# A hybrid decoder layer on one core: the recurrence's value projection by Strassen's scheme, with the copies of later stages moved

## The chip, the core and the metric

The kernel runs on one core of one Trainium2 chip. The metric is the device time of one execution, in microseconds (us). TensorE (PE) multiplies matrices; VectorE (DVE), ScalarE (ACT) and GpSimd (POOL) work on tiles; SyncE (SP) and POOL issue most of the DMA transfers. An L with a number is a line of the kernel before.

## The reference

One layer of a decoder: 512 tokens, 1024 channels, float32 throughout.

```
h  = RMSNorm(x)                          # 512 x 1024
P  = h @ W_in                            # one product, its columns split into
                                         #   q, f, i, z_a           (1024 each, recurrence)
                                         #   c_q, c_kv, k_rope, z_b (attention)
                                         #   g                      (2 x 1024, merge gates)
y_a = recurrence(q, f, v = i) * silu(z_a)        # 8 heads of 128, chunks of 32 tokens
y_b = latent attention(c_q, c_kv, k_rope) * silu(z_b)   # 8 heads, causal
m   = sigmoid(g_a) * (y_a @ W_pa) + sigmoid(g_b) * (y_b @ W_pb)
out = RMSNorm(x + m @ W_out)
```

The columns i of `W_in` give the recurrence's values: `v = h @ W_i`, 512 x 1024 by 1024 x 1024. This product is what the change rewrites.

## The kernel before, in words

**Products in three parts.** A float32 operand is held as two tiles: a high part, rounded to the type that PE multiplies fast, and a low part, what is left. A product is high x high, high x low and low x high, so three matmuls stand for one (mm3, L99). `hT` holds both parts of h, transposed. Weights come through `load_w` (L110): one DMA of 512 KB into one of three raw buffers, a cast on ACT for the high part (L129), and a subtraction on DVE for the low part (L130). There are four buffers for high parts and four for low parts, and three raw ones, so a load starts when the low part of the load three before it is done.

**The stages.** First x is normalised and transposed, and the small columns of attention are projected (the c stage, to L433; five transposed tiles `cT` and one `kpe` come out of it through PSUM banks of the pool `ax`, L422 to L432). Then come four pairs of recurrence heads (`hg_pair`, L585), then eight attention heads (L959), the two merge gates, the projection of y_a, the projection of y_b, and the output product. The gates, the projection of y_a and the output product already go by Strassen's scheme, in Winograd's form: seven products of quarter blocks instead of eight, paid for by sums of blocks.

**A recurrence pair** projects f (`proj_ch`, 48 matmuls), and both heads' decays, prefix products and keys follow on DVE and POOL (`hg_forget`, L459 to L490: on DVE a scaling, a scan, a reciprocal and three products a head). Pairs 0 and 2 then project 512 columns of values with `proj_tok` (L151, called on L603), 96 matmuls of 512 columns each: for each of four token tiles, eight slices of channels, three parts. A pair's values serve it and the next pair. Then come q, the gate z_a, the states, scores and outputs.

**Sums for Strassen's scheme.** `early_sums` (L816) makes four sums of blocks of h, half at a time, during pair 0: it adds the two parts of a block (L823), subtracts, splits into parts again and stores to DRAM (L830); the gates read them back much later (L1002). Sums of weight blocks are made in DRAM. A `BlockSums` copies four blocks of a weight matrix into DRAM tiles (`start`, L790; eight copies of 512 KB each for two gates, the projection of y_a and the output matrix, 32 in all) and adds other blocks onto them with accumulating DMAs from POOL (`add`, L795). The copies wait in the list `queued`; `load_w` takes one from it behind each plain load and issues it on SP (L124 to L126). The adds are taken one by one at calls of `step` (L845) from the list `adds` (L842).

**Order.** Except where a block says `manual_schedule`, a planner orders each engine's instructions ahead of time by readiness in its own model, with earlier program lines first; `issue_after` puts instructions behind a given one on its engine. On the chip each engine then works strictly in that order.

PSUM has eight banks: three in the pool `mm` and five in the pool `ax`.

Of the kernel before, what the change touches and what calls it, by code (L numbers as in the profile page):

```python
# [18 lines left out]
P = 128  # L19
D = 1024  # L20
# [18 lines left out]
def hybrid_layer(ctx: ExitStack, tc: tile.TileContext, a):  # L39
# [68 lines left out]
    queued = []  # L108

    def load_w(*pieces, to=None):  # L110
# [4 lines left out]
        for src in pieces:  # L115
# [6 lines left out]
            else:  # L122
                last_dma[0] = nc.sync.dma_start(raw[:, o : o + n].rearrange("p (k c) -> p k c", k=src.shape[1]), src)
# [4 lines left out]
            o += n  # L128
        last_hi[0] = nc.scalar.copy(hi[:, :o], raw[:, :o])  # L129
# [51 lines left out]
    kpe = Pair(cpool.tile([P, 2, S], F32R, "kpe")[:])  # L181
    cw = Pool("cwork", "right")
# [23 lines left out]
    x_sb = [st.tile([P, D], F32, "x", bufs=NT) for _ in range(NT)]  # L206
# [50 lines left out]
    def squares(t):  # L257
        sq = st.tile([P, D], F32, "sq", bufs=2)
        nc.scalar.activation(sq[:], x_sb[t][:], AF.Square, accum_out=rss[t][:, 0:1])
        power(rss[t][:, 0:1], rss[t][:, 0:1], 1.0 / D, EPS, neg_half[:, 0:1])  # L260
# [17 lines left out]
    def c_product(t, kh, kind, ks=range(4)):  # L278
# [3 lines left out]
        for k in ks:  # L282
            nc.tensor.matmul(ps, hT[l][:, 4 * kh + k, t * P : t * P + P], c_hl[kh][r][:, k * 256 : k * 256 + 256],  # L283
                             start=kh == 0 and kind == 0 and k == 0, stop=kh == 1 and kind == FIN and k == 3)

# [7 lines left out]
    with tc.manual_schedule(engines={mybir.EngineType.PE, mybir.EngineType.Activation, mybir.EngineType.DVE}):  # L293
# [49 lines left out]
        for t in range(1, NT):  # L343
            if t + 2 < NT:
                squares(t + 2)
            for kh in range(2):
                lo[kh]()
# [49 lines left out]
    c_second += [load_c2(j) for j in range(2, 4)]  # L397
    for t in range(NT):
# [4 lines left out]
        nc.scalar.copy(c_sb[:, t, 256:704], ps[:, 0:448])  # L403
    css = cw.tile([P, 2, NT], F32, "css")
# [31 lines left out]
    ya = ypool.tile([P, H, S], F32, tag="ya", name="ya")  # L436
    ma_pool = Pool("mla_a", "right")
    qtab = ma_pool.tile([P, 2, S], F32, "qtab")
    nc.gpsimd.dma_start(qtab[:], a["c_qtab"])
# [144 lines left out]

    def hg_pair(pair, in_forget=None, in_query=None, before_gate=None, last=None):  # L585
# [3 lines left out]
        if pair:  # L589
            step()  # L590
        else:
            early_sums(kh[0])
# [7 lines left out]
        if pair % 2 == 0:  # L600
            for t in range(NT):
                v_sb[t] = hw.tile([P, 512], F32, f"v{t}")
            proj_tok(w_in, COL_I + cc, hT, lambda t, ps: nc.scalar.copy(v_sb[t][:], ps[:]))  # L603
        else:
# [3 lines left out]
        step()  # L608
# [4 lines left out]
        if pair % 2 == 0:  # L613
# [156 lines left out]
    kh = [slice(0, 2), slice(2, 4)]  # L770
    half_t = [slice(0, 256), slice(256, 512)]
    blocks = lambda t: (t[:, 0:4, half_t[0]], t[:, 4:8, half_t[0]], t[:, 0:4, half_t[1]], t[:, 4:8, half_t[1]])
    TERMS = ((0, 0), (1, 1), (0, 1), (1, 0))

    def minus(out, x, y):
        nc.vector.tensor_tensor(out, x, y, op=ALU.subtract)

    def minus_minus(out, x, y):

        nc.vector.scalar_tensor_tensor(out, x, -1.0, y, op0=ALU.mult, op1=ALU.subtract)  # L780

    class BlockSums:
# [7 lines left out]
        def start(self):  # L790
            for t, ij in zip(self.t, TERMS):
                for q in kh:
                    queued.append(lambda t=t[:, q], w=self.w[ij][:, q]: nc.sync.dma_start(t, w))

        def add(self, *ns):  # L795
            with tc.issue_after(last_pool[0].ins):
                for n in ns:
                    x = {0: self.w[0, 1], 2: self.w[1, 1], 1: self.t[0], 3: self.t[1]}[n]
                    for q in kh:
                        nc.gpsimd.dma_start(self.t[n][:, q], x[:, q], accum_op=ALU.add)  # L800
# [13 lines left out]
    h_dram = [[dram.tile([P, 4, 256], F32, name=f"h{n}{i}") for i in range(2)] for n in range(1, 5)]  # L814

    def early_sums(q):  # L816

        E = lambda tag: ma_pool.tile([P, 2, 256], F32, tag)[:]
        h11, h12, h21, h22 = zip(*[[b[:, q] for b in blocks(t)] for t in hT])

        def whole(tag, hl):
            out = E(tag)
            nc.vector.tensor_tensor(out, hl[0].bitcast(F32), hl[1].bitcast(F32), op=ALU.add)  # L823
            return out

        def keep(n, tag, src):
            hl = Pair(ma_pool.tile([P, 2, 2, 256], F32R, tag)[:])
            split(*hl, src)
            for i in range(2):
                nc.sync.dma_start(h_dram[n - 1][i][:, q], hl[i].bitcast(F32))  # L830

# [428 lines left out]
```

## Time and profile before

| | us |
|---|---|
| median of 3 runs | 609.52 (609.49 to 610.1) |
| the profiled execution | 609.93 |
| its span, first to last instruction | 607.7 |
| PE busy in the span | 598.3 |
| DVE, ACT, POOL busy | 436.6, 286.2, 146.4 |

The span starts at 0 in all times below. The stages, as the trace has them: normalisation and c stage to 45 us, recurrence pairs from 45 to 281, attention from there to 407, the gates and the projection of y_a to 519, the projection of y_b to 562, the output product to 601. DMA moved 114.37 MB, 90 of them on the hardware queue that SP feeds and 22.6 on the software queue that POOL feeds.

### The profile page before, as it was taken

What the parts mean: (1) busy time and instruction counts of PE and PEld (TensorE: products, weight loads), DVE (VectorE), ACT (ScalarE), POOL (GpSimd) and SP (SyncE); (2) the same over time, 40 slices, a digit from 0 to 9 for tenths busy, and PEclk for the clock granted to TensorE, in tenths of its full rate; (3) what the DMA queues carried; (4) which work ended last, traced back from release to release, by engine and by line L of the source; (5) the groups of instructions that cost most, each with busy time, mean ns of one, the idle gap of its engine ahead of it and who ended that gap; (6) DMA issues with size and microseconds to landing.
All of it is one profiled execution on the core that took longest, in us unless ns stands there. A gap on an engine that the chain in (4) does not pass through costs nothing.

```text
span 607.7 us, 9766 instructions
## 1 busy us (share of the span) xinstructions
PE 598.3 (98%) x3670; PEld 524.8 (86%) x3670; DVE 436.6 (72%) x684; ACT 286.2 (47%) x533; POOL 146.4 (24%) x253
## 2 busy tenths in 40 slices
PE   8999999999999999999999999999999999999995
PEld 5998888888888888888888888899999999888884
DVE  7717989599764548959767776747757678567886
ACT  6555245333313342435646555438757854424452
POOL 3106322254350137414254530400000000000012
PEclk9999999999999999999999999999999999999998
DMA  7549479987969967573369575866665564695113
GB/s 257 177 138 345 154 218 369 320 220 171 237 151 275 220 185 147 125 172 90 57 163 169 148 152 126 237 243 198 189 184 178 195 195 160 200 347 183 61 35 139
DMA packets 74543, 114.37 MB, mean 188 GB/s; under 512 B 7512, under 2 KB 41726, under 8 KB 74496
## 3 DMA queue, kind: packets, MB, share of 16 engines
q1 hardware_dynamic: 65244, 89.95, 46.1%
q0 software_dynamic: 8336, 22.55, 19.9%
q10 hardware_dynamic: 916, 1.25, 0.6%
q8 instruction: 29, 0.48, 0.3%
q14 instruction: 18, 0.15, 0.1%
HBM read 105.34 MB, written 39.85 MB: 239 GB/s over the span
## 4 chain that ended last, share of the span: by engine, by line
PE 96%; ACT 1%; DMA 1%; DVE 0%; issue 0%; SPq 0%; POOLq 0%; POOL 0%; ACTq 0%
PE mm_ps L102 19%; PE mm_ps L104 19%; PE mm_ps L103 19%; PE ax_ps L898 16%; PE ax_ps L1096 5%; PE mm_ps L898 3%; PE mm_ps L283 2%; PE ax_ps L757 1%; PE ax_ps L731 1%; PE ax_ps L559 1%; PE mm_ps L1096 1%; PE ax_ps L561 1%; PE ax_ps L521 1%; DMA w_raw<-w_in 1%; PE ax_ps L104 1%; PE ax_ps L103 1%
## 5 line engine op out<-in xcount | busy, mean ns | idle before, releaser
L130 DVE TENSOR_TENSOR w_lo<-w_raw,w_hi 128x1024 fp32r<-128x1024 f32 (+3 forms) x116 | 138.3, 1205 | 68.3 <-ACT w_hi L129 65.4
L129 ACT CAST w_hi<-w_raw 128x1024 fp32r<-128x1024 f32 (+3 forms) x116 | 115.1, 1005 | 130.1 <-PE mm_ps L103 56.5
L102 PE MATMUL mm_ps<-hT,w_hi 128*128 128x512 f32 x320 | 125.8, 394 | 0.0
L103 PE MATMUL mm_ps<-hT,w_hi 128*128 128x512 f32 x320 | 125.3, 391 | 0.0
L104 PE MATMUL mm_ps<-hT,w_lo 128*128 128x512 f32 x320 | 125.2, 393 | 0.0
L104 PEld LDWEIGHTS mm_ps<-hT,w_lo 128*128 128x128 f32 x320 | 60.1, 188 | 12.3
L102 PEld LDWEIGHTS mm_ps<-hT,w_hi 128*128 128x128 f32 x320 | 60.2, 188 | 11.9
L103 PEld LDWEIGHTS mm_ps<-hT,w_hi 128*128 128x128 f32 x320 | 60.2, 188 | 11.9
L898 PE MATMUL ax_ps<-s,w_hi 128*128 128x256 f32 x384 | 54.2, 283 | 0.2 <-ACT w_hi L129 0.2
L898 PEld LDWEIGHTS ax_ps<-s,w_hi 128*128 128x128 f32 x384 | 49.6, 192 | 0.5 <-ACT w_hi L129 0.5
L1147 POOL TENSOR_SCALAR ssum<-ssum 128x1 f32<-128x1 f32 x3 | 0.9, 309 | 188.0 <-ACT sq L1134 188.0
L103 PE MATMUL mm_ps<-w_lo,hT 128*128 128x512 f32 (+1 forms) x96 | 36.6, 383 | 0.0
L104 PE MATMUL mm_ps<-w_hi,hT 128*128 128x512 f32 (+1 forms) x96 | 36.5, 382 | 0.0
L102 PE MATMUL mm_ps<-w_hi,hT 128*128 128x512 f32 (+1 forms) x96 | 36.2, 386 | 0.0
L739 ACT ACTIVATE p<-ax_ps,sm 128x128 f32<-128x128 f32 (+3 forms) x32 | 16.7, 525 | 35.4 <-DVE sm L738 32.8
L741 POOL TENSOR_SCALAR p<-p,sm 128x128 f32<-128x128 f32 (+3 forms) x28 | 15.6, 560 | 66.2 <-DVE sm L740 54.9
L898 PE MATMUL ax_ps<-s,w_lo 128*128 128x256 f32 x192 | 31.4, 284 | 0.0
L469 DVE RECIPROCAL tf<-pr 128x512 f32<-128x512 f32 x8 | 26.8, 3348 | 0.1
L898 PEld LDWEIGHTS ax_ps<-s,w_lo 128*128 128x128 f32 x192 | 26.6, 192 | 0.2 <-DVE w_lo L130 0.2
L102 PE MATMUL mm_ps<-cT,w_hi 128*128 128x512 f32 x52 | 20.7, 397 | 0.0
L104 PEld LDWEIGHTS mm_ps<-w_hi,hT 128*128 128x128 f32 x96 | 18.0, 188 | 3.0
L102 PEld LDWEIGHTS mm_ps<-w_hi,hT 128*128 128x128 f32 x96 | 18.0, 188 | 2.9
(308 smaller groups left out, 1204.8 us busy)
## 6 DMA issues: line engine op xcount, KB each, us to landing
w_raw<-w_in SPq DMA_DIRECT2D x54, 512.0 KB, 6.4
g_t<-w_in SPq DMA_DIRECT2D x16, 512.0 KB, 9.1
w_raw<-g_t SPq DMA_DIRECT2D x16, 512.0 KB, 4.4
g_t<-w_in POOLq DMA_DIRECT2D x8, 512.0 KB, 10.5
pa_t<-w_proj_a SPq DMA_DIRECT2D x8, 512.0 KB, 8.9
g_t<-g_t POOLq DMA_DIRECT2D x8, 512.0 KB, 9.5
out_t<-w_out SPq DMA_DIRECT2D x8, 512.0 KB, 8.0
s<-h POOLq DMA_DIRECT2D x8, 512.0 KB, 11.6
```

The costliest lines, as they stand in the source:

```text
L102: nc.tensor.matmul(ps, lh[lsl], rh[rsl], start=start, stop=False)
L103: nc.tensor.matmul(ps, lh[lsl], rl[rsl], start=False, stop=False)
L104: nc.tensor.matmul(ps, ll[lsl], rh[rsl], start=False, stop=stop)
L129: last_hi[0] = nc.scalar.copy(hi[:, :o], raw[:, :o])
L130: last_lo[0] = nc.vector.tensor_tensor(lo[:, :o], raw[:, :o], hi[:, :o].bitcast(F32), op=ALU.subtract)
L283: nc.tensor.matmul(ps, hT[l][:, 4 * kh + k, t * P : t * P + P], c_hl[kh][r][:, k * 256 : k * 256 + 256], start=kh == 0 and kind == 0 and k ...
L469: nc.vector.reciprocal(rp[:], pr[:])
L521: nc.tensor.matmul(sps[:, sl], kt_[:, sl], v_sb[i][:, (h % 4) * P : (h % 4) * P + P], start=True, stop=True)
L739: last_act[0] = nc.scalar.activation(p[:, :n], sps[:, :n], AF.Exp, scale=SCALE, bias=sm[:, 1:2], accum_out=sm[:, 2:3])
L741: scaled_p = (nc.vector if final else nc.gpsimd).tensor_scalar(p[:, :n], p[:, :n], sm[:, 3:4], 0.5, op0=ALU.mult, op1=ALU.mult)
L898: nc.tensor.matmul(ps[:, o], w[k // 2][i][:, k % 2, cols], ap[j][:, k], start=not banks and c == 0 and n == 0, stop=n == 11, skip_group_ch ...
L1096: nc.tensor.matmul(ps[:, o : o + n], ap[i][:, k, t * P : t * P + P], w[k // 2][j][:, k % 2, o : o + n], start=fresh and c == 0, stop=c == ...
```

## The change: what it does

**Values.** `v = h @ W_i` goes by the same form of Strassen's scheme: h in four blocks of 256 tokens by 512 channels, W_i in four of 512 by 512. `v_product` is one of its seven products: two token tiles, each with 12 matmuls of 512 columns. Pair 0 runs five of them (`values_first`), which give all tokens of the first 512 columns and four partial tiles (`v_late`) that are kept in SBUF; pair 2 runs the other two (`values_rest`). The first partial sum `u` accumulates over four products in two banks of `ax`; before, the values used banks of `mm`.

**Sums of h.** `early_sums` runs once, on whole blocks, in the c stage, behind the last low part of that stage. Sums 2 and 3 stay in SBUF for pair 0, sums 1 and 4 are stored by POOL's queue at once and fetched again for pair 2. Stores of sums 2 and 3 join `queued`.

**Sums of W_i.** Two are made in SBUF, in the buffer of y_a: four loads on SP, two accumulating DMAs on POOL and two additions on DVE in the c stage, two additions on DVE in pair 0, and for pair 2 two more loads and two accumulating DMAs (`RestSum`). x, at the start, lies in that buffer too.

**Transfers.** The 32 copies join `queued` at the end of pair 0's values, behind four stores; after pair 0 six fetches go ahead of them. Two entries go behind each load up to pair 1, one from pair 2 on. The adds for the y_a projection and the output matrix go into attention; the last two heads before the final one issue two steps each. The table `qtab` is loaded after pair 2.

**Order in pairs.** Pairs 1 to 3 project z_a before q; only pair 0 has it after the states.

The core of the diff:

```diff
-                if queued:
+                for _ in range(min(len(queued), behind[0])):
                     with tc.issue_after(last_dma[0].ins):
                         queued.pop(0)()
...
-    x_sb = [st.tile([P, D], F32, "x", bufs=NT) for _ in range(NT)]
+    x_sb = [ya[:, 2 * t : 2 * t + 2].rearrange("p k c -> p (k c)") for t in range(NT)]
...
+    def save(n, q, hl):
+        (nc.gpsimd if n in (1, 4) else nc.sync).dma_start(h_dram[n - 1][:, :, q], hl.both.bitcast(F32))
...
+        e22, e21, e11 = whole("e22", h22), whole("e21", h21), whole("e11", h11)
+        minus(e22, e22, e21)
+        keep(1, e22)
+        minus_minus(e22, e22, e11)
+        s2 = keep(2, e22)
+        minus(e21, e11, e21)
+        s3 = keep(3, e21)
+        e12 = whole("e12", h12)
+        minus_minus(e12, e12, e22)
+        keep(4, e12)
...
+    for q in kh:
+        nc.sync.dma_start(i_w3[:, q], i_w[0, 1][:, q])
+    for q in kh:
+        nc.gpsimd.dma_start(i_w3[:, q], i_w[1, 1][:, q], accum_op=ALU.add)
+    for q in kh:
+        nc.sync.dma_start(i_w2[:, q], i_w[0, 0][:, q])
...
+    with tc.issue_after(c_lo_last.ins):
+        s_kept = early_sums()
+        for q in kh:
+            nc.vector.tensor_tensor(i_w2[:, q], i_w2[:, q], i_w3[:, q], op=ALU.add)
...
+    def v_product(ap, w, done, banks=None, tile=ax_tile):
+
+        res = banks or [tile() for _ in range(2)]
+        for t, ps in enumerate(res):
+            for n, (x, k) in enumerate((x, k) for x in range(3) for k in range(4)):
+                i, j = ((0, 0), (1, 0), (0, 1))[x]
+                nc.tensor.matmul(ps[:], ap(i, k, t), w[k // 2][j][:, k % 2], start=not banks and n == 0, stop=n == 11,
+                                 skip_group_check=banks is not None)
+            done(t, ps)
+        return res
...
+        u = v_product(h11, i_block(0, 0), lambda t, ps: nc.scalar.copy(v_sb[t][:], ps[:]))
+        v_product(s2, i_split(i_w2), late(2), u)
+        v_product(s3, i_split(i_w3), late(3), u)
+        w10, raws = [], []
+        for q in kh:
+            w10.append(load_w(i_w[1, 0][:, q]))
+            nc.vector.tensor_tensor(i_w2[:, q], i_w2[:, q], last_raw[0].rearrange("p (k c) -> p k c", k=2), op=ALU.add)
+        v_product(h12, w10, lambda t, ps: nc.vector.tensor_tensor(v_sb[t][:], v_sb[t][:], ps[:], op=ALU.add), tile=mm_tile)
+        v_product(h22, i_split(i_w2), lambda t, ps: nc.scalar.copy(v_sb[2 + t][:], ps[:]), u)
+        for n, hls in zip((2, 3), s_kept):
+            for q, hl in zip(kh, hls):
+                queued.append(lambda n=n, q=q, hl=hl: save(n, q, hl))
+        for w in (*gate_w, pa_w, out_w):
+            w.start()
...
+        r = v_product(of_sum(s_late[1]), i_split(i_w2), rest(3), tile=mm_tile)
+        v_product(of_sum(s_late[4]), i_block(1, 1), rest(2), r)
...
-            proj_tok(w_in, COL_I + cc, hT, lambda t, ps: nc.scalar.copy(v_sb[t][:], ps[:]))
-        else:
+            (values_rest if pair else values_first)()
+        if pair:
             zz = gate()
...
+    adds = [(gate_w[0], 0), (RestSum(),), (gate_w[0], 1), (gate_w[0], 2), (gate_w[0], 3), (gate_w[1], 0), (gate_w[1], 1),
+            (gate_w[1], 2), (gate_w[1], 3), None, (pa_w, 0), (pa_w, 1), (pa_w, 2), (pa_w, 3),
+            (out_w, 0), (out_w, 1), (out_w, 2), (out_w, 3)]
...
     for pair in range(H // 2 - 1):
+        if pair == 2:
+            behind[0] = 1
         hg_pair(pair)
         if pair == 0:
-            early_sums(kh[1])
+            fetch_rest()
     early = []
+    qtab = ma_pool.tile([P, 2, S], F32, "qtab")
+    nc.gpsimd.dma_start(qtab[:], a["c_qtab"])
...
-            step()
+            for _ in range(1 + (h > 4)):
+                step()
```

`rest(n)` finishes a tile of values on DVE, straight from the bank: minus the bank, plus the kept partial tile.

More of the change, by code (lines that the diff above doesn't have):

```diff
@@ L284, in c_product, with minus, minus_minus, kept @@
                              start=kh == 0 and kind == 0 and k == 0, stop=kh == 1 and kind == FIN and k == 3)
+    kh = [slice(0, 2), slice(2, 4)]
+    half_t = [slice(0, 256), slice(256, 512)]
+    blocks = lambda t: (t[:, 0:4, half_t[0]], t[:, 4:8, half_t[0]], t[:, 0:4, half_t[1]], t[:, 4:8, half_t[1]])
+    TERMS = ((0, 0), (1, 1), (0, 1), (1, 0))
+    def minus(out, x, y):
+        nc.vector.tensor_tensor(out, x, y, op=ALU.subtract)
+    def minus_minus(out, x, y):
+        nc.vector.scalar_tensor_tensor(out, x, -1.0, y, op0=ALU.mult, op1=ALU.subtract)
+    h_dram = [dram.tile([P, 2, 4, 256], F32, name=f"h{n}") for n in range(1, 5)]
+    i_v = w_in[:, COL_I : COL_I + D].rearrange("(k p) c -> p k c", p=P)
+    i_w = {(i, j): i_v[:, 4 * i : 4 * i + 4, 512 * j : 512 * j + 512] for i in range(2) for j in range(2)}
+    i_w3, i_w2 = ya[:, 0:4], ya[:, 4:8]
+    KEEP = {1: ("qn", "kn"), 2: ("qn", "kn"), 3: ("qp", "qtab"), 4: ("qp", "qtab")}
+    def kept(n):
+        return [Pair(ma_pool.tile([P, 2, 2, 256], F32R, tag)[:]) for tag in KEEP[n]]
+    def save(n, q, hl):
+        (nc.gpsimd if n in (1, 4) else nc.sync).dma_start(h_dram[n - 1][:, :, q], hl.both.bitcast(F32))
+    def early_sums():
+        es = Pool("early", "left")
+        h11, h12, h21, h22 = zip(*[blocks(t) for t in hT])
+        def whole(tag, hl):
+            out = es.tile([P, 4, 256], F32, tag)[:]
+            nc.vector.tensor_tensor(out, hl[0].bitcast(F32), hl[1].bitcast(F32), op=ALU.add)
+            return out
+        def keep(n, src):
+            hls = kept(n) if n in (2, 3) else [Pair(es.tile([P, 2, 2, 256], F32R, f"s{i}")[:]) for i in range(2)]
+            for q, hl in zip(kh, hls):
+                split(*hl, src[:, q])
+                if n in (1, 4):
+                    save(n, q, hl)
+            return hls
+        e22, e21, e11 = whole("e22", h22), whole("e21", h21), whole("e11", h11)
[8 more added lines that the diff above has]
+        keep(4, e12)
+        es.close()
+        return s2, s3
     w_c1 = w_in[:, COL_C + 256 : COL_C + 704].rearrange("(k p) c -> p k c", p=P)
@@ L345, in hybrid_layer @@
                 squares(t + 2)
-            for kh in range(2):
-                lo[kh]()
+            for n in range(2):
+                lo[n]()
             if t + 1 < NT:
@@ new lines, in hybrid_layer, with add, fetch_rest @@
+    s_late = {}
+    class RestSum:
+        def add(self):
+            with tc.issue_after(last_pool[0].ins):
+                for q in kh:
+                    nc.gpsimd.dma_start(i_w2[:, q], i_w[0, 1][:, q], accum_op=ALU.add)
+    def fetch_rest():
+        items = [lambda q=q: nc.sync.dma_start(i_w2[:, q], i_w[0, 0][:, q]) for q in kh]
+        for n in (1, 4):
+            s_late[n] = kept(n)
+            for q, hl in zip(kh, s_late[n]):
+                items.append(lambda n=n, q=q, hl=hl: nc.sync.dma_start(hl.both.bitcast(F32), h_dram[n - 1][:, :, q]))
+        queued[0:0] = items
@@ L612, in hg_pair @@
             before_gate()
-        if pair % 2 == 0:
+        if not pair:
             zz = gate()
```

92 lines of the change are left out of this document (46 added, 46 removed).

## The prediction

> **What bounds the kernel now.** I read the page's busy times first, then the chain that ended last, then what PE waited for.
>
> ```profile
> PE 598.3 (98%) x3670; PEld 524.8 (86%) x3670; DVE 436.6 (72%) x684; ACT 286.2 (47%) x533; POOL 146.4 (24%) x253
> ...
> PE 96%; ACT 1%; DMA 1%; DVE 0%; issue 0%; SPq 0%; POOLq 0%; POOL 0%; ACTq 0%
> ```
>
> ```profile
> PE ax_ps L248 <- DVE zero L294: 1.2, 1, 1.2
> PE mm_ps L283 <- ACT hT L274: 0.6, 1, 0.6
> PE ax_ps L898 <- ACT w_hi L129: 0.2, 1, 0.2
> PE ax_ps L272 <- DVE xn L264: 0.2, 1, 0.2
> ```
>
> PE is the bound: it works 98% of the span, the chain is 96% PE, and its waits on other engines are 2.2 us together. So time falls only by matmuls taken away, and each microsecond for which PE is made to wait comes back in full. Next, the windows of the pairs (span, then busy time of PE, PEld, DVE, ACT, POOL, then the granted clock, the DMA engines' busy share and GB/s; the boundaries lie at each pair's outputs), and two stretches inside them.
>
> ```profile
> 54.00:113.50 59.50, 59.50 (x352) 49.70 (x351) 53.16 (x70) 23.87 (x36) 18.11 (x29) 1.00 0.83 261
> 113.50:160.30 46.80, 46.80 (x302) 39.62 (x301) 37.00 (x43) 14.58 (x33) 20.61 (x38) 1.00 0.89 229
> 160.30:218.30 58.00, 58.00 (x352) 48.68 (x351) 36.86 (x43) 19.14 (x38) 15.93 (x34) 1.00 0.92 229
> ```
>
> ```profile
> 58.20:80.50 22.30, 22.30 (x102) 18.38 (x101) 22.30 (x26) 8.60 (x13) 7.29 (x18) 1.00 0.48 169
> 82.00:122.00 40.00, 40.00 (x266) 33.85 (x265) 29.60 (x43) 15.20 (x33) 13.07 (x12) 1.00 1.05 328
> ```
>
> PE never pauses here. But in pair 0 DVE has 53.16 us of work in 59.5, and while the first values run (58.2 to 80.5) it has no free moment. ACT has less than half. The DMA engines are full from 82 to 122 and PE does not notice. So what the change asks of DVE in pair 0 matters most, then what it asks of the DMA engines.
>
> **What is taken from PE.** Before, the values are 2 x 96 = 192 matmuls of 512 columns (`proj_tok`, four token tiles by eight slices by three parts). After, seven products of 24, 168. The price comes from a run of 24 such matmuls, 512 columns wide, in the output product:
>
> ```profile
> 562.41 5.44 PE ax_ps L1096 x24
> ```
>
> That is 0.227 us each, 5.44 us a product. A matmul's own row shows 0.39 us because neighbours overlap; 96 of them at 0.227 give 21.8 us, which with four transposes fills the 22.3 of the window above. The 24 matmuls fewer are 5.44 us. Nothing is added on PE. Pair 0's values become 27.2 us instead of 21.8, pair 2's 10.9 instead of 21.8.
>
> **Sums of h, moved to the c stage.** The rows of DVE there (start, duration, and in brackets the idle time before):
>
> ```profile
> 42.97 3.50 DVE L130 TENSOR_TENSOR w_lo<-w_raw,w_hi 128x1024 fp32r<-128x1024 f32 x3 [12.19 <-ACT w_hi L129]
> 49.29 1.23 DVE L130 TENSOR_TENSOR w_lo<-w_raw,w_hi 128x1024 fp32r<-128x1024 f32 x1 [2.82 <-ACT w_hi L129]
> 50.44 2.59 DVE L421 TENSOR_SCALAR c_sb<-c_sb,css 128x384 f32<-128x384 f32 x8
> 53.65 1.23 DVE L130 TENSOR_TENSOR w_lo<-w_raw,w_hi 128x1024 fp32r<-128x1024 f32 x1 [0.61 <-ACT w_hi L129]
> 54.79 0.54 DVE L464 TENSOR_SCALAR f<-tf,c,c 128x512 f32<-128x512 f32 x1
> 56.22 1.23 DVE L468 TENSOR_TENSOR_SCAN pr<-f,fr 128x512 f32<-128x512 f32 x1 [0.89 <-POOL fr L465]
> 57.37 0.73 DVE L427 SCALAR_TENSOR_TENSOR cT<-ax_ps,par,cT 128x512 fp32r<-128x512 f32 x1
> 58.01 3.34 DVE L469 RECIPROCAL tf<-pr 128x512 f32<-128x512 f32 x1
> 61.27 2.63 DVE L427 SCALAR_TENSOR_TENSOR cT<-ax_ps,par,cT 128x512 fp32r<-128x512 f32 x4
> 63.81 1.22 DVE L130 TENSOR_TENSOR w_lo<-w_raw,w_hi 128x1024 fp32r<-128x1024 f32 x1
> 64.94 0.69 DVE L486 TENSOR_TENSOR ki<-k,tf 128x512 f32<-128x512 f32 x1
> 65.55 0.69 DVE L823 TENSOR_TENSOR qr<-hT,hT 128x512 f32<-128x512 f32 x1
> 66.15 0.69 DVE L823 TENSOR_TENSOR qs<-hT,hT 128x512 f32<-128x512 f32 x1
> 66.75 0.69 DVE L823 TENSOR_TENSOR qh<-hT,hT 128x512 f32<-128x512 f32 x1
> 67.35 0.68 DVE L823 TENSOR_TENSOR p<-hT,hT 128x512 f32<-128x512 f32 x1
> 67.96 0.68 DVE L172 TENSOR_TENSOR kpe<-ax_ps,kpe 128x512 fp32r<-128x512 f32 x1
> ```
>
> Two operands of 1024 elements cost 1.17 us in a row (3.50 for three), of 512 elements 0.60 (65.55 to 66.15). The sums are eight operations of 1024 and eight low parts of 512, and two additions of weights follow: 10 x 1.17 + 8 x 0.60 = 16.5 us. DVE stands idle for the 12.19 us before 42.97, so they start near 30.8 and end near 47.3. The eight casts on ACT, at 0.6 each, lie beside. The first projection's low parts, begun at 42.97 before, then begin at 47.3, and the first is there at 48.4:
>
> ```profile
> 46.01 0.40 PE L104 MATMUL mm_ps<-hT,w_lo 128*128 128x512 f32 x1
> ...
> 58.22 0.39 PE L102 MATMUL mm_ps<-w_hi,hT 128*128 128x512 f32 x1
> ```
>
> PE uses that low part at 46.01, so it could stand 2.4 us; or it does its 16 matmuls on the high part first (3.6 us, to 48.7) and nothing is lost. DVE's later idle time (2.82 and 0.61) absorbs the shift. The old sums leave pair 0: 24 operations of 512, 14.4 us of DVE's work there.
>
> POOL issues the stores of sums 1 and 4 itself. Those of sum 4 fall due near 46 and may stand ahead of the roots for which L421 waits:
>
> ```profile
> L800 POOL DMA_DIRECT2D g_t<-w_in x8 | 9.7, 1436 | 0.0
> ```
>
> Two issues at 1.44 put L421 off by up to 2.9 us, from 50.4 to 53.3. That costs nothing as long as DVE is on low parts until 52.0 (47.3 + 4 x 1.17) anyway; without that cover the transposes of the c tiles, next on PE, come up to 2.9 late, inside the bound of the next part.
>
> **DVE's account in pair 0.** A head's six steps on DVE are in the rows above: 0.54 (L464), 1.23 (L468), 3.34 (L469) and three products at 0.69 (L486).
>
> A head is 7.2 us. From 47.3 without a pause: four low parts (f and the first product) 4.7, L421 2.6, cT 3.4, kpe 0.6, two heads 14.4, and eight more low parts and two additions for the products two to five, 10 x 1.17 = 11.7. That is 37.4 us, so the last low part is there at 84.7. PE's plan: values from 58.2, a product each 5.44, four transposes of 0.45, so the fifth starts at 80.4; its 11th matmul is the first that needs that part, 2.3 us in: 82.7. DVE is late by about 2 us, and PE waits for it. The bounds: if both heads go before the third product's weights, these are ready at 47.3 + 25.7 + 4.7 = 77.7, needed at 69.5 + 2.3 = 71.8, and PE loses 6; if the second head goes behind them, 0. The row at 63.81, a low part between the first head's steps, shows that weights do slip ahead; I take the balance of the whole account, 2.0.
>
> A second way to the same wait: the first product now opens a bank of `ax`. All five hold the transposed c tiles until DVE has read them (L427), and kpe's transposes want the first to come free. By the rows 57.37, 58.01 and 61.27 a second bank comes free at 61.9, behind a reciprocal: 3.7 us after 58.2. If the four reads go before the reciprocal it is about 58.7. PE waits once, and DVE goes on meanwhile, so this and the low parts do not add; the larger counts, and 0 to 6 holds for both.
>
> **Pair 2.** A bank of `values_rest` must be read by DVE before the second product may add to it, 2.7 us after its last matmul. A reciprocal of 3.34 before the 0.68 of the read makes it 1.3 late: 0 to 1.3, and I take 0.5. DVE's 36.86 of 58.0 us become, with four reads of 0.68, 39.6 of 47.1; that fits. ACT gets six casts of weights more in the kernel, beside its 47%: nothing. In attention POOL issues 16 accumulating DMAs instead of 12, and POOL is busy 24%: nothing on the path.
>
> **Transfers.**
>
> ```profile
> q1 hardware_dynamic: 65244, 89.95, 46.1%
> q0 software_dynamic: 8336, 22.55, 19.9%
> ```
>
> So 512 KB (0.524 MB) takes 0.461 x 607.7 x 0.524 / 89.95 = 1.63 us of all 16 engines on SP's queue, and 2.81 on POOL's. In the c stage four loads, two accumulating transfers and four stores from POOL, 4 x 1.63 + 6 x 2.81 = 23.4 us, take the place of three copies (4.9):
>
> ```profile
> 30.80:42.97 12.17, 12.17 (x62) 11.29 (x61) 0.00 (x0) 5.62 (x17) 0.00 (x0) 1.00 0.47 166
> ```
>
> ```profile
> 28.03 0.39 SPq L123 DMA_DIRECT2D w_raw<-w_in  x1
> ```
>
> Half of the DMA engines' time is free there. SP may issue the four loads ahead of the first projection's, which then land up to 6.5 us later (4 x 1.63). The second of those was asked for at 28.03, and PE begins with the first at 45, so I take nothing; were one late, its whole delay would be PE's. The full stretch 82:122 cost PE nothing either, so I take 0 of a range up to 6.0 (below).
>
> **The sum.** On the profiled execution: 609.93 - 5.44 + 2.0 + 0.5 = 607.0. It lies 0.41 above the median of the runs, 609.52, so the forecast for the median is 606.6.
>
> **Rivals.** *All covers hold.* The planner puts the second head behind the weights and the reads before the reciprocal. For: no PE wait in any pair before, with DVE full. Time 609.52 - 5.44 = 604.1.
>
> *DVE swallows the gain.* Heads first, as earlier lines go first: a wait of 4.3 to 6.6 us with pair 2's share, 608.3 to 610.8, no change, near 609.5. For: DVE works without a pause from 58.2 to 80.5 already, and it trails its work there: kpe's low part runs at 67.96, though its cast on ACT ended at 62.2. Against: 63.81.
>
> ```profile
> 61.59 0.59 ACT L171 CAST kpe<-ax_ps 128x512 fp32r<-128x512 f32 x1 [2.36 <-PE ax_ps L431]
> ```
>
> *Loads stand behind copies in pair 1: slower.* Pair 1 has six loads, and two entries go behind each: 18 x 1.63 + 6 accumulating x 2.81 = 46.2 us of DMA in 46.8 us of PE. For the pair before the same account gives 12 x 1.63 + 16.9 = 36.5, and the row shows 0.89 x 46.8 = 41.7, so 1.14 times as much; 52.8 then, 6.0 over. If the last loads wait for all of it, with DVE's 2.5 in other pairs: 609.52 - 5.44 + 2.5 + 6.0 = 612.6. It decides once loads come more than 4.2 us late altogether. Against: three raw buffers let a load start long before use, and the stretch at 1.05 did no harm. [...]
>
> ```profile
> w_raw<-w_in SPq DMA_DIRECT2D x54, 512.0 KB, 6.4
> ```
>
> That is 6.4 us from issue to landing where 1.63 is its own transfer. [...]
>
> **How the numbers follow.** A measurement of this kernel can tell about 0.2%, 1.2 us, from no change. Forecast, a PE wait of 1 to 4.2 us (605.1 to 608.3): 0.40. All covers hold: 0.25. DVE swallows it: 0.19. Loads late: 0.16. Faster is the first two, 0.65; same 0.19; slower 0.16. The range leaves out the lower edge of the cover case and the upper part of the slow one: 603.9 to 611.0.
>
> **What would show it.** Right: 168 matmuls of the values in the matmul groups, PE's busy time down by about 5; DVE without idle time from 31 to 85; a PE wait of 1 to 4 us between 58 and 85 put down to a low part (DVE) or to the release of a bank, none in pair 1; DMA share near 1 in pair 1. Wrong: PE waits in pair 1 or 2 on w_raw, by way of ACT's casts; a c stage that ends later than 45; or PE without any wait, which would mean that DVE's order put weights first.

## The result: slower, 619.5 us against 609.5

The changed kernel takes 619.51 us (median; 618.15 to 621.69) where the kernel before takes 609.52 (609.49 to 610.1). The ratio is 1.0166, interval 1.0155 to 1.0178. The forecast was 606.6, in a range of 603.9 to 611.0. The profiled execution after is 619.51 us, its span 617.7 against 607.7. From here on an L with a number is a line of the kernel whose rows are shown; the changed kernel's L132, for instance, is L130 before.

First the page of the changed kernel (busy times, granted clock by slices of 15.4 us, the chain), then all that PE waited for.

```profile
PE 599.4 (97%) x3646; PEld 524.2 (85%) x3646; DVE 449.8 (73%) x692; ACT 291.0 (47%) x539; POOL 158.3 (26%) x261
...
PEclk9999699999999999998999999999999999999998
...
PE 79%; DMA 6%; DVE 5%; POOL 3%; issue 3%; ACT 2%; SPq 1%; POOLq 0%; ACTq 0%; DVEq 0%
```

```profile
PE ax_ps L496 <- DVE c_sb L492: 2.9, 1, 2.9
PE ax_ps L102 <- DVE k L634: 2.7, 1, 2.7
PE ax_ps L502 <- DVE cT L498: 1.8, 1, 1.8
PE ax_ps L252 <- DVE zero L354: 1.2, 1, 1.2
PE ax_ps L588 <- ACT kt L580: 0.8, 1, 0.8
PE mm_ps L104 <- DVE w_lo L132: 0.8, 1, 0.8
PE ax_ps L664 <- DVE cT L498: 0.6, 1, 0.6
```

The 24 matmuls are gone (3670 to 3646), yet PE is busy 1.1 us longer: it ran some of the others at a lower clock, in slices 5 and 19 (0.6 and 0.8 in the line PEclk). The chain is 79% PE where it was 96%. The waits stand in two places. The windows of the pairs, cut at their outputs as in the prediction:

```profile
54.00:128.20 74.20, 68.81 (x375) 56.68 (x374) 54.42 (x64) 27.10 (x37) 16.62 (x38) 0.93 0.68 233
128.20:176.50 48.30, 47.49 (x304) 39.95 (x303) 34.09 (x43) 14.93 (x32) 21.93 (x38) 1.00 0.76 183
176.50:228.90 52.40, 52.40 (x327) 44.45 (x326) 40.33 (x48) 17.95 (x36) 18.37 (x35) 1.00 0.91 244
```

PE stood idle for 5.4 us of pair 0's window, at a mean clock of 0.93; for 0.8 in pair 1's, and not at all in pair 2's. PE's rows with a wait (in brackets) show where: the first of them still ahead of that window, the other three, 5.4 together, in it. The rows of POOL and DVE show why. There kd holds the rotary products of attention's shared key, and css the roots by which DVE scales the c tiles (c_sb):

```profile
46.51 0.50 PE L104 MATMUL mm_ps<-hT,w_lo 128*128 128x512 f32 x1 [0.79 <-DVE w_lo L132]
61.03 1.97 PE L496 MATMUL ax_ps<-ident,c_sb 128*128 128x128 f32 x8 [2.94 <-DVE c_sb L492]
64.83 1.09 PE L502 MATMUL ax_ps<-ident,kd 128*128 128x128 f32 x4 [1.83 <-DVE cT L498]
66.53 3.78 PE L664 MATMUL ax_ps<-w_hi,hT 128*128 128x512 f32 x8 [0.62 <-DVE cT L498]
```

```profile
46.03 5.71 POOL L485 TENSOR_TENSOR kd<-c_sb,ktab 128x256 f32<-128x256 f32 x1 [6.55 <-ACT c_sb L470]
...
56.67 1.11 POOL L179 TENSOR_TENSOR css<-css,fixed 128x4 f32<-128x4 f32 x1
```

```profile
49.85 1.28 DVE L174 TENSOR_TENSOR s<-e,s 128x512 fp32r<-128x512 f32 x2
51.26 1.56 DVE L132 TENSOR_TENSOR w_lo<-w_raw,w_hi 128x1024 fp32r<-128x1024 f32 x1
55.69 1.55 DVE L492 TENSOR_SCALAR c_sb<-c_sb,css 128x384 f32<-128x384 f32 x4 [2.87 <-POOL css L179]
57.16 1.21 DVE L174 TENSOR_TENSOR w_lo<-ya,w_hi 128x1024 fp32r<-128x1024 f32 x1
58.29 3.46 DVE L492 TENSOR_SCALAR c_sb<-c_sb,css 128x256 f32<-128x256 f32 x4
```

The same kd product and the roots in the kernel before:

```profile
45.90 1.17 POOL L414 TENSOR_TENSOR kd<-c_sb,ktab 128x256 f32<-128x256 f32 x1 [27.84 <-ACT c_sb L403]
...
49.25 2.30 POOL L177 TENSOR_TENSOR css<-css,fixed 128x4 f32<-128x4 f32 x2
```

From kd's start to the second root POOL took 5.7 us before and takes 11.8 now. DVE is through with its sums and low parts at 52.8, then stands 2.87 us for the roots, which POOL works out behind kd. The scaling of the c tiles ends at 61.75, so their transposes, and all behind them on PE, come late. And PE is at half clock when it starts again (windows; the last three numbers are granted clock, DMA share, GB/s):

```profile
62.00:64.00 2.00, 1.00 (x5) 0.59 (x3) 2.00 (x3) 1.27 (x2) 0.00 (x0) 0.50 0.14 57
...
70.00:72.00 2.00, 2.00 (x7) 1.58 (x7) 1.97 (x2) 0.23 (x1) 0.72 (x6) 0.68 0.00 0
```

The second place is the start of attention. The rows of SP's queue show out_t's copies among the loads, two issues held for 5.3 and 4.1 us (0.37 when free); ACT then waits 9.60 us for a load, its squares come late, and PE waits for k, again with half clock behind it:

```profile
259.30 5.29 SPq L124 DMA_DIRECT2D w_raw<-w_uq  x1
264.63 4.12 SPq L937 DMA_DIRECT2D out_t<-w_out  x1
```

```profile
272.59 1.04 ACT L131 CAST w_hi<-w_raw 128x1024 fp32r<-128x1024 f32 x1 [9.60 <-DMA w_raw<-w_in]
```

```profile
282.00:284.00 2.00, 0.85 (x2) 0.75 (x3) 0.73 (x2) 1.64 (x6) 1.57 (x3) 0.72 0.04 12
284.00:286.00 2.00, 2.00 (x6) 1.41 (x6) 2.00 (x6) 0.00 (x0) 0.00 (x0) 0.50 0.00 0
```

The account of the span: 24 matmuls, -5.44; the four waits above, 0.79 + 2.94 + 1.83 + 0.62 = +6.2; half clock from 61 to 71.5 (some 6.5 us of PE's work at about 0.50, 2 us at 0.68), +3.9; pair 1, +0.8; attention, +2.7 for the wait and +1.5 of clock. Together +9.7 of the 10.0 measured.

### The profile page after: what moved, and what is told of

Same layout as the page of the kernel before. It is cut to its first block, busy times and chain, and to the rows that moved or that the text cites. A ratio compares the mean times of both kernels' runs of the same rounds, so it can differ in the third digit from the quotient of the medians.

```text
span 617.7 us, 9737 instructions
## 1 busy us (share of the span) xinstructions
PE 599.4 (97%) x3646; PEld 524.2 (85%) x3646; DVE 449.8 (73%) x692; ACT 291.0 (47%) x539; POOL 158.3 (26%) x261
## 4 chain that ended last, share of the span: by engine, by line
PE 79%; DMA 6%; DVE 5%; POOL 3%; issue 3%; ACT 2%; SPq 1%; POOLq 0%; ACTq 0%; DVEq 0%
PE ax_ps L1019 16%; PE mm_ps L102 12%; PE mm_ps L103 12%; PE mm_ps L104 12%; PE ax_ps L1218 5%; PE ax_ps L664 4%; PE mm_ps L664 3%; PE mm_ps L1019 2%; DMA w_raw<-w_in 2%; PE mm_ps L287 2%; DMA out_t<-w_out 2%; PE ax_ps L882 1%; PE ax_ps L908 1%; DVE w_lo L132 1%; DMA w_raw<-g_t 1%
## 5 line engine op out<-in xcount | busy, mean ns | idle before, releaser
L132 DVE TENSOR_TENSOR w_lo<-w_raw,w_hi 128x1024 fp32r<-128x1024 f32 (+3 forms) x114 | 134.5, 1193 | 71.7 <-ACT w_hi L131 62.6
L131 ACT CAST w_hi<-w_raw 128x1024 fp32r<-128x1024 f32 (+3 forms) x114 | 112.7, 1004 | 130.2 <-PE mm_ps L103 55.0
L533 POOL TENSOR_SCALAR k<-tf,c1n,c 128x512 f32<-128x512 f32 x8 | 13.1, 1633 | 37.9 <-ACT tf L530 37.9
L102 PE MATMUL mm_ps<-cT,w_hi 128*128 128x512 f32 x52 | 20.9, 402 | 0.0
L103 PE MATMUL mm_ps<-cT,w_hi 128*128 128x512 f32 x52 | 20.4, 393 | 0.0
L104 PE MATMUL mm_ps<-cT,w_lo 128*128 128x512 f32 x52 | 20.3, 391 | 0.0
L1019 PE MATMUL ax_ps<-hT,w_hi 128*128 128x256 f32 x128 | 18.0, 283 | 0.0
L569 POOL TENSOR_TENSOR q<-qi,gh 128x256 f32<-128x256 f32 x8 | 8.6, 1124 | 36.6 <-DVE qi L568 36.6
```

What stands on the lines that cost most here:

```text
L102: nc.tensor.matmul(ps, lh[lsl], rh[rsl], start=start, stop=False)
L103: nc.tensor.matmul(ps, lh[lsl], rl[rsl], start=False, stop=False)
L104: nc.tensor.matmul(ps, ll[lsl], rh[rsl], start=False, stop=stop)
L132: last_lo[0] = nc.vector.tensor_tensor(lo[:, :o], raw[:, :o], hi[:, :o].bitcast(F32), op=ALU.subtract)
L533: nc.gpsimd.tensor_scalar(k[:], tf[:], c1n[:, h : h + 1], c1[:, h : h + 1], op0=ALU.mult, op1=ALU.add)
L1019: nc.tensor.matmul(ps[:, o], w[k // 2][i][:, k % 2, cols], ap[j][:, k], start=not banks and c == 0 and n == 0, stop=n == 11, skip_group_ch ...
```

## The experiments

Three theories for the two places, and a fourth, D, that came up later:
- A: POOL's kd product is held up by DVE's operations with two operands from SBUF, and with it the roots.
- B: DVE has too much work due ahead of the first values (the prediction's own mechanism); what POOL does is secondary.
- C: copies left for the start of attention hold up its loads.
- D: transfers crowd pairs 1 and 2.

Landmarks of the profiled executions help: the start of the outputs' first matmul (`hg_out`, L626) in pair 0 and pair 3, called the first and the fourth hg_out. In the kernel before they are 113.3 and 265.4, after 128.2 and 271.2 (the changed kernel has five of the seven products of the values in pair 0, so the first compares only among changed kernels).

**Roots ahead of kd (roots_first).**

```
+    with tc.issue_after(roots.ins):     # roots = the second power(css ...)
         nc.gpsimd.tensor_tensor(kd[:, :, 0, :], kr, ktab[:, :, 0, :], op=ALU.mult)
```

> The changed kernel, with one order on POOL turned round: the rope products of the shared key (five operations, the first took 5.71 us in the changed kernel against 1.17 before) go behind the roots of the c stage, which DVE's scaling of the c tiles and so PE's transposes wait for. Theory A (POOL's long product holds the roots back, and PE's idle time then also halves its clock): the roots start near 47 instead of 53.6, the scaling is done before 57, PE's waits between 56 and 67 fall from about 6 us to 2 or less, PEclk stays 1.00 in 62 to 72, and the time falls by 6 to 9 us, to 611 to 613. Theory B (the prediction's: DVE has too much work there, whatever POOL does; the banks of ax come free late because of it): the roots move but the scaling and the reads of the banks stay within 1 to 2 us of where they were, and the time falls by less than 3 us.

Measured: 614.47 us (610.23 to 617.44), ratio 1.0071 [1.0048, 1.0094]. The scaling starts at 53.4 instead of 55.7, the first hg_out stands at 124.4. About half of the loss goes: less than A said, more than B. (The rows are of an execution of 617.44 us, 3.0 above the median.) But the first root, four elements wide, was now the one held:

```profile
48.63 3.59 POOL L178 TENSOR_SCALAR css<-css 128x4 f32<-128x4 f32 x1 [8.36 <-ACT csq L479]
```

A wait of 2.4 us for cT's low part at the kd transposes remained. So A has a share and B is not excluded.

**Without the slower pace from pair 2 on (two_behind).**

```
-        if pair == 2:
-            behind[0] = 1
```

> The changed kernel, with two queued transfers behind each load in pairs 2 and 3 as well, so that the 32 copies are through before attention. Theory C (the copies left over for the start of attention hold up the loads there: ACT waits for a load from 263 to 272.6, starts the four turning DMAs late and with them the squares of the last pair, and PE stands 2.7 us at 280 and then runs at half clock): the wait near 280 goes, and the time falls by 3 to 5 us; the early waits near 60 stay as they are. Rival: the copies come at a bad place anywhere, and pair 2 or 3 gets the wait instead; same time within 1 us.

Measured: 616.73 us, ratio 1.0122 [1.0092, 1.0151]. SP's queue has no copy left at 255 us and the start of attention is whole again:

```profile
272.00:282.00 10.00, 10.00 (x64) 9.05 (x63) 3.49 (x5) 5.26 (x20) 2.44 (x4) 1.00 0.51 130
```

That is C. From the fourth hg_out to the end the changed kernel takes 346.5 us, this one 341.9 (the kernel before 342.3). The time falls by 2.8 only, since a wait of 2.7 us for asb (L626) is new at the end of pair 1; the chain leads from it back to an accumulating transfer for the values of pair 2 that was 11.5 us on its way.

This run shows one thing more. Up to pair 2 its source is the changed kernel's, with the c stage's rows in the same order, and yet its first hg_out stands at 125.7, 2.5 us earlier. POOL's rows for kd and the second root:

```profile
46.05 1.10 POOL L485 TENSOR_TENSOR kd<-c_sb,ktab 128x256 f32<-128x256 f32 x1 [6.46 <-ACT c_sb L470]
...
54.56 1.11 POOL L179 TENSOR_TENSOR css<-css,fixed 128x4 f32<-128x4 f32 x1
```

Here kd took 1.10 us beside the same work of DVE; the operations behind it were held instead, and the roots were there at 55.7 in place of 57.8 (51.6 in the kernel before). So the 5.71 us of kd are of one execution, the delay of the roots is of both, and a difference of 2.5 us at the first hg_out can come from the execution alone.

**Is it the two operands? (before_adds, before_recip).** The kernel before, with extra work on DVE in the c stage: 16 additions of 128x1024, or 6 reciprocals of 128x512 (20 us), whose results nobody uses.

```
+        for _ in range(16):   # or 6 x nc.vector.reciprocal(dum[:, 0:512], hT ...)
+            nc.vector.tensor_tensor(dum[:], hT[0][:, 0:2] ..., hT[1][:, 0:2] ..., op=ALU.add)
```

> The kernel before, with 16 additions of two SBUF operands of 1024 elements put on DVE in the c stage, behind the last low part there (16 x 1.17 = 18.7 us of DVE's time; their result is used by nobody; the sums of h stay in pair 0, the values unchanged). Theory A (two-operand work on DVE keeps POOL's two-operand products from SBUF): POOL's first rope product, 1.17 us before, takes 3 us or more, and the roots behind it come late. Theory B: it stays at 1.2 to 1.5 us, and any PE wait comes from DVE's queue alone.

> The same as the run with 16 additions, but with 6 reciprocals of 512 elements (one operand, 3.35 us each, 20.1 us of DVE's time) in their place. Theory A: POOL's first rope product stays near 1.2 us while DVE is as full as with the additions, apart from the low parts of weights between them. Theory B: the same PE waits as with the additions, since DVE is busy as long.

Measured: 613.47 and 609.72 (one run each; before 609.68). POOL's rows with additions, then with reciprocals:

```profile
45.13 1.18 POOL L420 TENSOR_TENSOR kd<-c_sb,ktab 128x256 f32<-128x256 f32 x1 [27.83 <-ACT c_sb L404]
46.27 1.45 POOL L421 TENSOR_TENSOR kt<-c_sb,ktab 128x128 f32<-128x128 f32 x1
```

```profile
45.40 0.74 POOL L419 TENSOR_TENSOR kd<-c_sb,ktab 128x256 f32<-128x256 f32 x1 [27.84 <-ACT c_sb L404]
46.09 0.46 POOL L420 TENSOR_TENSOR kt<-c_sb,ktab 128x128 f32<-128x128 f32 x1
```

Beside additions and low parts the kt products took three times as long (1.45 and 1.44 us), beside a reciprocal no longer than in the kernel before (0.46 and 0.47). From kd's start to the second root POOL took 8.4 us with additions, 5.5 with reciprocals and 5.7 in the kernel before. So DVE's work on two tiles held POOL up here, and its reciprocals on one did not. A's own sign, a kd of 3 us or more, failed all the same: kd took 1.18 us, as before. How long POOL is held the rows do not settle: 5.71 us spans six of DVE's instructions, back to back, and 3.59 four. DVE can be the one held, too: in two_behind, where kd took 1.10, DVE's low part of 512 columns beside it took 1.23 instead of 0.68, and in before_adds one of 1024 beside kd and kt took 1.77, where two in a row had taken 2.36.

**Roots away from POOL (roots_act).**

```
+        nc.scalar.activation(css[:, i, :], css[:, i, :], AF.Sqrt, scale=1.0 / n, bias=eps)
+        nc.vector.reciprocal(css[:, i, :], css[:, i, :])
```

> The changed kernel with one edit: the roots of the c norms are taken by ScalarE (square root) and VectorE (reciprocal of 4 elements) instead of GpSimd's power; the kd products stay on GpSimd. [...] Theory A (GpSimd's products are held up by VectorE's two-operand work and so the roots come late): the c_sb scaling starts within 1 us of the fourth sum's low parts instead of 2.9 us behind them, the three waits of PE between 54 and 70 us (2.9, 1.8, 0.6) come down to 2 us or less together, the clock is at 0.9 or more in 62:72, and the time is 611.5 to 613.5. Theory B (VectorE has too much to do, the c tiles give their banks back late): the wait of L502 for cT's low part stays at about 2 us, as it did with the roots put first, and the time stays at 614 to 616. The loss at the start of attention is untouched under either.

Measured: 617.9 us, ratio 1.0145 [1.0111, 1.0178], slower than either theory said. The scaling ran without a pause from 54.15 to 57.9, but the wait for cT's low part became 3.3 us, and the one at the start of attention 3.9. The first hg_out at 125.0 is no better than with the roots put first. With the roots off POOL it is DVE's own work that stands in the way, which is B's part: two low parts and an addition of weights (57.86 to 61.47) go ahead of the first read of a c tile.

**The fourth sum and the additions for i_w2 later (late_sum, late_pace, late_two).**

```
+    with tc.issue_after(kpe_low.ins):   # behind kpe's low part
+        (the two i_w2 additions)
+        fourth_sum()                    # e12, minus_minus, keep(4)
```

late_pace sets two transfers behind each load again from pair 3 on, late_two all through.

> The changed kernel with the roots ahead of the kd products on GpSimd, and with the fourth sum (about 3.5 us of VectorE) and the two additions for i_w2 (2.3 us) put behind kpe's low part instead of ahead of the c_sb scaling. No work is removed. Theory A: VectorE is then free when the roots fall due, so the roots take well under 1 us each, the waits of PE between 54 and 72 us are under 2 us together with the clock at 0.95 or more, and the time is 610.5 to 612.5 (what remains over 604 is the start of attention, about 4.3, and the small waits of pairs 0 to 2). Theory B: the same VectorE work is only moved some 15 us, onto the low parts and sums that the first two products need, so waits of 3 us or more appear ahead of the values (66 to 90 us) and the time is 614 to 618.

> late_sum, and two queued transfers again behind each load from pair 3 on (one in pair 2 only), so that fewer copies are left for the start of attention. Theory C (copies still queued on SyncE at 259 to 270 us hold up the loads there): the wait of about 2.7 us near 283 us and the half clock behind it go, and the time is 3 to 4.5 below late_sum's, 606.5 to 609. Against C: copies brought forward only hold up pair 3's loads; the time is within 1 us of late_sum's.

> late_sum, and two queued transfers behind each load all through (pair 2 is not paced down). Theory C: as in the run that did this alone, nothing is left for the start of attention and the windows there are full; the time is 3 to 4.5 below late_sum's, 606.5 to 609, and equal to late_pace's within 1. Against: the wait of 2.7 us for asb in pair 1 that stood in that run comes back, and the time is 609 to 611.

Measured: 624.99 (ratio 1.0249 [1.0233, 1.0264]), 632.77 (1.0379 [1.0353, 1.0404]) and 621.5 (1.0194 [1.0177, 1.0211]). PE is whole from 46 to 62 and the first values start at 57.9 instead of 66.5, so the c stage is cured. But the same work now lies ahead of what the second and fourth products need:

```profile
68.50 0.88 PE L671 MATMUL ax_ps<-w_hi,qn 128*128 128x512 f32 x2 [4.86 <-ACT v L701]
...
83.49 2.07 PE L671 MATMUL mm_ps<-w_hi,hT 128*128 128x512 f32 x4 [4.92 <-ACT w_hi L131]
```

```profile
66.34 1.14 ACT L173 CAST s<-e 128x512 fp32r<-128x512 f32 x2 [1.60 <-DVE e L301]
67.39 0.59 ACT L537 ACTIVATE tf<-mm_ps 128x512 f32<-128x512 f32 x1
67.88 1.06 ACT L701 COPY v<-ax_ps 128x512 f32<-128x512 f32 x2
```

In ACT's order the copy of v that releases the bank stood behind the casts of the fourth sum, and those waited for DVE. A's expectation (610.5 to 612.5) fails and B's direction holds, though the time lies above B's 614 to 618 as well: the work needs another stage, not another place in this one. Between these three, two transfers behind each load are worth 3.5 us once more (C); late_pace, which brings the copies back in pair 3, lost 9 us of PE between 230 and 260, so that middle way is worse than both.

**The fourth sum in pair 0, behind the queries (sum4, sum4_two, sum4_kd_first).** It is formed from the kept second sum and h12. In the first two kernels one operand has the wrong sign (h12 - s2 in place of -h12 - s2); what they give is wrong there, but the work is the same (0.68 us an operation either way).

```
-        e12 = whole("e12", h12); minus_minus(e12, e12, e22); keep(4, e12)
+            with tc.issue_after(last_dve[0].ins):   # pair 0, behind hg_query
+                fourth_sum()
```

> The changed kernel with the roots ahead of the kd products on GpSimd, and with the fourth sum worked out only in pair 0 behind the queries, from the kept second sum and h12 (8 operations of 512 columns, about 5.4 us of VectorE there, 2.0 us more than before in all), where VectorE was busy 15 of 30 us. The two additions for i_w2 stay where they are. Theory B (too much VectorE work due ahead of the first values; 3.5 us of it was the fourth sum): the waits of PE between 46 and 100 us, 5.3 us with the roots alone put first and 9.8 with the sum moved to 59 to 72 us, come down to 3 or less, the first hg_out stands at 121 to 123.5 us (124.4 with the roots first), and the time is 610 to 613; what is left is the start of attention. If only GpSimd's place mattered (theory A alone), the fourth sum's place changes nothing: 613.5 to 615.5.

> The kernel above, with two queued transfers behind each load all through, so that no copy is left for the start of attention. Theories B and C together: the time is 3 us below the kernel above, 606.5 to 609.5, at last at or below the kernel before. Against: the wait in pair 1 that came with this pacing (2.7 us for asb) comes back, and it is 609 to 612.

> The changed kernel with one edit alone: the fourth sum is worked out in pair 0 behind the queries; GpSimd keeps the kd products ahead of the roots, as the change has it. If GpSimd's order costs something by itself even when VectorE has the fourth sum off its hands (theory A beside B), the first hg_out stands at 120 to 124 us against 117.7 with the roots first, and the time is 615 to 618. If the fourth sum's place is the whole cause (B alone), the first hg_out stands within 1 us of 117.7 and the time within 1.5 us of the kernel with both, 612.5 to 615.5.

Measured: sum4 613.91 us (ratio 1.0074 [1.0045, 1.0102]), sum4_two 611.28 (1.0043 [1.0017, 1.007]), sum4_kd_first 614.8 (1.0087 [1.0074, 1.01]). sum4 has its first hg_out earlier than B said (121 to 123.5), but its time lies in A's 613.5 to 615.5 and not in B's 610 to 613; sum4_two lies in the range that went with a wait in pair 1 (2.7 us, though not for asb); sum4_kd_first has its first hg_out in neither range (119.1, against 120 to 124 and 116.7 to 118.7), its time in B's. The last completes a square of two edits on the changed kernel:

| | kd first: first / fourth hg_out, time | roots first |
|---|---|---|
| fourth sum in the c stage | 128.2 / 271.2, 619.5 | 124.4 / 267.5, 614.5 |
| fourth sum in pair 0 | 119.1 / 267.2, 614.8 | 117.7 / 265.8, 613.9 |

At the first hg_out the sum's place is worth 9.1 us alone and 6.7 beside the other edit; POOL's order 3.8 alone, 1.4 beside. With two_behind's 125.7 in the first corner, the same program so far, it is 6.5 and 1.3 alone. So the sum's place is worth more than executions differ by, POOL's order not surely, and that the two multiply each other is not shown. With the sum away the roots were there at 53.2 even at POOL's old order. So up to the first hg_out B's work is the larger cause. In the whole time the two edits come out alike: 4.7 and 5.0 us alone, and 0.6 and 0.9 as the second of the two, which the intervals cannot tell from nothing. With both, PE has no wait from 46 to the first hg_out:

```profile
54.00:117.70 63.70, 63.70 (x365) 53.05 (x364) 51.65 (x62) 26.21 (x38) 14.78 (x34) 1.00 0.53 181
117.70:168.70 51.00, 48.03 (x298) 40.15 (x297) 36.36 (x43) 16.52 (x34) 18.44 (x37) 0.97 0.91 262
```

But the second row, of the same kernel (sum4), shows the other half: of 10.5 us won at the first hg_out only 5.4 are left at the fourth. Pair 1 now loses 3 us. In sum4_two the chain and SP's queue name the cause:

```profile
123.45 16.02 DMA w_raw<-w_in
```

```profile
123.45 1.12 SPq L124 DMA_DIRECT2D w_raw<-w_in  x1
124.61 5.40 SPq L948 DMA_DIRECT2D g_t<-w_in  x2
130.11 3.96 SPq L124 DMA_DIRECT2D w_raw<-w_in  x1
```

```profile
60.00:70.00 10.00, 10.00 (x46) 8.27 (x45) 9.78 (x9) 5.59 (x8) 3.48 (x11) 1.00 0.00 1
100.00:105.00 5.00, 5.00 (x27) 4.21 (x26) 5.00 (x11) 1.07 (x2) 0.00 (x0) 1.00 0.00 0
115.00:140.00 25.00, 23.50 (x122) 19.67 (x120) 13.74 (x14) 8.07 (x22) 7.96 (x18) 1.00 1.08 340
```

A load takes 16 us among copies while a share of 1.08 says that the DMA engines are full, and in two stretches before that they had stood idle. That is theory D.

**Copies put where the DMA engines idle (sum4_early, sum4_early_a).** Four of the first gate's copies go right behind the loads for the third block of weights; sum4_early adds three behind pair 1's first load, ahead of the fetches of h's sums for pair 2. The sign is right from here on.

```
+        with tc.issue_after(last_dma[0].ins):
+            for _ in range(4):
+                queued.pop(0)()
```

> The last kernel (roots first, fourth sum in pair 0, two transfers behind each load), with copies put where the DMA engines idle: four of the first gate's copies right behind the loads for the third product (the share of the DMA engines was 0.00 at 60 to 70 us), and three more behind pair 1's first load (0.00 at 100 to 105). Each moves 512 KB there and back; seven of them leave the stretch of 110 to 230 us, where the share was 1.0 and over and PE lost about 5.6 us to loads, one of which took 16 us. Theory D (what is left of the loss is transfers crowded into pairs 1 and 2): the waits of PE between 130 and 230 us come down from 5.6 to 2.5 or less and the time is 606 to 609, below the kernel before. Against D: the waits there are not from transfers, or the early copies hold up the values' loads; the time is 610.5 to 613. The fourth sum has its sign right in this kernel.

> The kernel above with the four early copies alone; the three behind pair 1's first load are left out. Theory D: the time lies between the two, 607.5 to 610.5, with about half of the waits between 130 and 230 us left. Against D: no difference to the kernel without them, 610.5 to 612.

Measured: sum4_early 610.16 us (604.64 to 612.81), ratio 1.0008 [0.9986, 1.003]; sum4_early_a 607.75 (607.43 to 608.66), ratio 0.9973 [0.9963, 0.9984]. The second beats both kernels, the one before by 0.3%, and came as expected; the first missed its 606 to 609 and varied most of all. PE's waits in the faster one, but for the 1.2 us of the start and two of 0.3 and 0.2:

```profile
PE mm_ps L102 <- ACT tf L528: 2.2, 1, 2.2
PE ax_ps L640 <- DVE k L632: 1.5, 1, 1.5
```

D is borne out only in part. The share at 115 to 140 is still 1.08 in sum4_early_a, with a wait of 2.2 us there. In the traced execution of sum4_early pair 1 has no wait at all, at a share of 1.05 from 136 to 156, and pair 2 has two, 2.7 us together. So a full share does not make PE wait by itself.

**Which copies, and POOL's order once more (early_a_kd, early_a_one2, early_a_one1).** sum4_early_a with kd first again; with one transfer behind each load from pair 2 on; with one in pair 1 and two after.

> The fastest kernel so far (fourth sum in pair 0, two transfers behind each load, four early copies) without the roots put first. By A beside B: 609 to 612, with waits for cT or c_sb between 46 and 70 us. By B alone: 607 to 608.5.

> The fastest kernel so far with the change's own pacing again (one transfer behind each load from pair 2 on). There the copies were all issued by 205 us, and the DMA engines' share was 0.95 at 160 to 200 and 0.7 to 0.8 at 200 to 260. Theory D (crowding): the copies spread to 240 us, the wait of 1.5 us for k in pair 2 goes, none is left for the start of attention at 260 us, and the time is 605.5 to 607.5. Against: copies reach the start of attention again as in the change (theory C), and it is 609 to 611.

> The fastest kernel so far with one transfer behind each load in pair 1 alone, and two from pair 2 on. Theory D: the share of 1.05 in 130 to 160 comes down, the wait of 2.2 us at 141 (for a load that stood behind copies) goes, and the time is 604.5 to 607. Against: what pair 1 does not copy, pairs 2 and 3 have to, waits of the same size come there or at the start of attention, and it is 607.5 to 611.

Measured: 609.76 (1.0012 [0.9998, 1.0026]), 610.58 (1.001 [1.0001, 1.0018]) and 611.46 us (1.0039 [1.0024, 1.0055]). POOL's order is worth 2.0 us here, as A beside B says, with a wait of 1.3 us for cT. Both other expectations of D fail. With one behind from pair 2 on, attention's start is whole, and yet PE waits 3.0 us in pair 1 instead of 2.2, at the same pace there, and runs at a clock of 0.60 and 0.54 from 140 to 148, where sum4_early_a had 1.00. With one behind in pair 1 that wait falls to 0.6, and others of 3.0 and 1.1 us come in pair 2. So the copies can be moved but not made to vanish; why the same pair 1 waits 2.2 us in one kernel and 3.0 in another stays open.

## Why the prediction was wrong, point by point

- **-5.44 for the matmuls:** the 24 are gone; with the waits mended, sum4_early_a runs 1.9 us below the kernel before with 3.7 us of waits in pairs 1 and 2.
- **DVE's account:** its first half was right. The sums start at 29.8 (30.8 forecast), and the last of them and of the low parts that slipped between ends at 52.8 (52.0). An operation of 1024 costs what was said (3.49 us for three in a row; 3.50 in the kernel before).
- **"That costs nothing as long as DVE is on low parts until 52.0 anyway": this step failed.** It counted two issues of POOL ahead of the roots, which came behind them (57.74), and took all else on POOL at its durations of before. Beside DVE's back-to-back sums and low parts POOL took 11.8 us instead of 5.7 from kd to the second root (9.6 in two_behind), the roots were there at 57.8 (51.6 in the kernel before), and the scaling ended at 61.75 where 54.6 was in the account. The cost came in the c stage, as two waits of 2.94 and 1.83 us, not at the fifth product, where none stands. The sum's +2.0 for DVE's low parts should have been +6.2, 0.79 of it for the first projection's low part, which was taken as nothing. Taking POOL out of it does not bring the account back: in roots_act the scaling still ended at 57.9, and DVE's work held the c tiles.
- **A bank of `ax` held by a c tile:** right as a mechanism (1.83 us for L498 at the kd transposes, 0.62 at the first product), inside its bound of 3.7. Here it comes from the late c stage, not from a reciprocal.
- **The clock was not priced at all.** With PE whole in the kernel before there was no row for it; it cost some 3.9 us in pair 0 and 1.5 in attention.
- **Pair 2, +0.5:** no wait there.
- **"In attention ... nothing on the path":** wrong. The accumulating transfers were priced, the copies left on SP's queue were not: 2.7 us and the clock, and 2.6 to 3.5 us less in the three pairs of runs that took them away (two_behind, late_two, sum4_two).
- **The rivals:** *DVE swallows the gain* has its direction, not its size. *Loads stand behind copies in pair 1* did not happen in the changed kernel (share 0.76, no wait on a load there); it happened as soon as PE came on time, in sum4 and sum4_two, at shares of 1.07 and 1.08 from 115 to 140 where the changed kernel has 0.85. That the late start of pair 0 had covered it fits this and was not tested by itself. *All covers hold*, 604.1, was reached by no median.

## What to carry to other kernels

Work put into the idle time of an engine still meets the other engines at its end: ask who waits for that engine's next result, and what its neighbour has to read meanwhile. A sum that is needed two stages later belongs in the stage that has slack, not in the first gap that holds it. When a repair moves the bound earlier, look at what was covered by the delay (here the crowded transfers) before counting the gain. And look at a second execution before taking one row's duration for the price of an edit.

## What was not expected of the hardware

GpSimd can lose more than one VectorE instruction's time: in roots_first 3.59 us went to an operation of four elements (0.47 for two in the kernel before) beside four VectorE operations on two tiles, back to back (two of 1.2 us and two of 0.6); in before_recip the kt products lost nothing beside a reciprocal of 3.35 (0.46 and 0.47, as in the kernel before). How much it loses differed between two executions with the same work beside it: kd took 5.71 us in the changed kernel and 1.10 in two_behind.

VectorE's scalings, which have one tile as input, can be slowed too. The eight took 2.59 us in the kernel before, and 3.74 and 3.79 in sum4_kd_first and roots_act, where POOL's memsets ran beside them; the last four alone took 3.46 in the changed kernel, with memsets until 60.82, but also 2.58 in sum4_two, beside POOL's products and no memset. What POOL has to run for this was not tested.

Half clock (0.50) can follow a short wait and stay away after a longer one. After 2.57 us of wait in sum4_kd_first PE had 0.50 in the window 144 to 146; after 3.11 us at the same place in early_a_kd it kept 1.00:

```profile
144.00:146.00 2.00, 2.00 (x6) 1.55 (x5) 2.00 (x3) 0.49 (x1) 0.62 (x2) 0.50 1.04 383
```

```profile
144.00:146.00 2.00, 2.00 (x10) 1.63 (x9) 2.00 (x4) 0.48 (x2) 1.62 (x2) 1.00 1.07 366
```

What decides between the two, these runs do not show.
